# The filter taps' rests, last samples and sums as products of 128 rows and 128 columns

## The chip, the core and the metric

The kernel runs on one core of one Trainium2 chip. The metric is the device time of one execution in microseconds, as the median of several runs. The engines are named as in the profile: PE is TensorE's matrix products, PEld its weight loads, DVE is VectorE, ACT ScalarE, POOL GpSimd, and SP the queue that starts most of the DMAs.

## The reference: what is computed

The program is one layer with two half feed-forward blocks and two token mixers between them. The change touches the Hyena mixer's filters: a small network gives, for each of 512 positions, two orders and two directions, 512 channels. They are windowed, the second direction is turned round, and the whole is divided by its sum of absolute values over all positions.

```python
def hyena_kernels(l, w1, b1, fr1, w2, b2, fr2, w3):
    t, z = hyena_pos_features(l)
    h = jnp.sin(fr1 * (z @ w1 + b1))
    h = jnp.sin(fr2 * (h @ w2 + b2))
    h = (h @ w3).astype(jnp.float32).reshape(l, HYENA_ORDER, 2, B_WIDTH)
    ...
    h = h * window[:, None, None, :]
    kern = jnp.concatenate([h[:, :, 0], jnp.flip(h[:, :, 1], axis=0)], axis=0)
    return kern / (jnp.sum(jnp.abs(kern), axis=0, keepdims=True) + HYENA_L1_EPS)
```

Everything else (the feed-forward blocks, the recurrence, the convolution itself) is the same before and after.

## The kernel before

**Numbers in two parts.** Nearly every product is made from operands that are split into a rounded part (`hi`, made by ACT at line 127) and the rest (`lo`, made by DVE at line 128). `mm3` (lines 255 to 258) multiplies hi by hi, hi by lo and lo by hi. In the profile's rows a product reads `out<-moving,stationary`, then the stationary block's rows and columns, then the moving operand's rows and columns.

**The filter generator.** `filters()` makes four passes, one for each half of the channels (256) and each order. The last network layer has only 64 inputs, so its two parts lie one below the other in one tile: rows 0 to 63 of `h2s` are the rounded part of the activations and rows 64 to 127 their rest. The weights `w3r` are loaded twice, below each other, and rounded to `w3h`. So one product of 128 rows gives (hi + rest) times `w3h` (line 671). The weights' own rest `w3l` is only made for rows 0 to 63 (line 661), and a second product of 64 rows adds hi times `w3l` (line 672). Positions are dealt out to four quarters: position 4m + j is column m of `h2s[:, j]`, shifted by 4.

Each pass goes through four quarters. A quarter has four products of `taps` (two directions, lines 671 and 672 each), into one PSUM buffer `ps_w` (written `ps("ps_w3")` in the code). DVE multiplies them by the window (`hw`, line 679), POOL forms sum and difference of the two directions (`pm`, lines 683 and 684), ACT takes absolute values (line 685), POOL adds them up in `ab` (line 689; the buffer's name in the rows is `hw`), and the quarter before is split into `ahi` and `alo`.

The second direction is shifted by one position, so that its last sample (position 511) falls off the four quarters. After the quarters it is made apart: the two products again with a single stationary column (`slice(131, 132)`), which give one row `pl[0:1]` (`ps_last`). DVE multiplies it by the window's last row (line 698), ACT takes the absolute value (line 699): `la`, one row.

The column sum (lines 703 and 704) multiplies `ab` by a block of ones, and adds `la` by a product of one row. DVE inverts it, and the transform of the taps follows (`ps_k`, 36 products of 128 rows and 256 columns per pass, with the table `ft` stationary).

**The order.** The kernel is written as generators that yield a guess of their cost. A `Clock` interleaves `filters()` with the first feed-forward block, `ffn0()`, whose products (`ps_gl`, `ps_gc`, `ps_dl`, `ps_dc`) fill the time in which the vector engines work on a quarter. A scheduler then orders each engine's instructions, with a time model of its own. All PSUM tiles rotate through eight buffers; `la` and `wl` are tiles of the group `c1`, which rotates through seven.

After `ffn0()` come the context's norm (`context_norm`, lines 393 to 423), woven into the projections of the mixers (`ps_w`).

Of the kernel before, what the change touches and what calls it, by code (L numbers as in the profile page):

```python
# [10 lines left out]
F32 = mybir.dt.float32  # L11
# [4 lines left out]
ALU = mybir.AluOpType  # L16
# [3 lines left out]
P = 128  # L20
# [63 lines left out]
def layer_kernel(ctx: ExitStack, tc: tile.TileContext, a: dict, out: bass.AP):  # L84
    nc = tc.nc
    V, A, G, PE = nc.vector, nc.scalar, nc.gpsimd, nc.tensor
# [4 lines left out]
    mx = ctx.enter_context(tc.tile_pool(name="mx", bufs=1))  # L91
# [4 lines left out]
    def ps(name):  # L96
        return psp.tile([P, 512], F32, tag="ps", name=name, bufs=8)
# [16 lines left out]
    def c2(name, dims, dt=F32):  # L114
        return mx.tile([P] + dims, dt, tag="c2", name=name, bufs=15)
# [4 lines left out]
    def load(dst, src):  # L120
        nc.sync.dma_start(out=dst, in_=src)
# [4 lines left out]
    def split(hi, lo, x, eng=V):  # L126
        A.copy(hi, x)  # L127
        return eng.tensor_tensor(out=lo, in0=x, in1=hi.bitcast(F32), op=ALU.subtract)  # L128

    def raw_tile(name):  # L130
        return wp.tile([P, 1024], F32, tag="wraw", name=name, bufs=3)
# [144 lines left out]
    ones = const.tile([P, P], F32, name="ones")  # L276
# [11 lines left out]
    h2s = const.tile([P, 4, 132], F32R, name="h2s")  # L288
# [349 lines left out]
    def filters():  # L638
        ftab = forward_table()
        worder = [(hh, q) for hh in range(2) for _ in range(2) for q in range(4)]  # L640

        def window():
            win = c2("win", [2, 256])
            load(win, a["win"][worder.pop(0)])
            return win

        for hh, o in ((0, 0), (0, 1), (1, 0), (1, 1)):
            cs = slice(hh * 256, hh * 256 + 256)
            raw = raw_tile("w3r")
            w3r = raw[:, 0:512].rearrange("p (d c) -> p d c", d=2)  # L650
            for half in range(2):
                load(w3r[64 * half:64 * half + 64], a["hy_w3"][:, 2 * o:2 * o + 2, cs])
            hyb = c1("hyb", [256])
            load(hyb, a["hy_bias"][o, cs].partition_broadcast(P))
            wl = mx.tile([1, 256], F32, tag="c1", name="wl", bufs=7)
            load(wl, a["win_last"][:, cs])
            win = window()
            yield 0.0, 5.0
            w3h, w3l = (c2(n, [2, 256], F32R) for n in ("w3h", "w3l"))
            A.copy(w3h, w3r)  # L660
            V.tensor_tensor(out=w3l[0:64], in0=w3r[0:64], in1=w3h[0:64].bitcast(F32), op=ALU.subtract)
            V.tensor_scalar_mul(out=hyb, in0=hyb, scalar1=1.0 / 512.0)
            yield 0.0, 1.5
            ahi, alo = (c8(n, [2, 4, 256], F32R) for n in ("ahi", "alo"))
            ab = late = None

            def taps(p_, q, d, last=False):

                j, m = (q, 4) if d == 0 else ((q + 3) % 4, 4 - (q == 0))
                t = slice(131, 132) if last else slice(m, m + P)  # L670
                PE.matmul(p_, h2s[:, j, t], w3h[:, d], start=True, stop=False)
                PE.matmul(p_, h2s[0:64, j, t], w3l[0:64, d], start=False, stop=True)

            for q in range(4):
                p_ = ps("ps_w3")
                taps(p_[:, 0:256], q, 0)
                taps(p_[:, 256:512], q, 1)
                hw = c2("hw", [2, 256])
                V.tensor_tensor(out=hw, in0=p_.rearrange("p (d c) -> p d c", d=2), in1=win, op=ALU.mult)
                if q < 3:  # L680
                    win = window()
                pm = c2("pm", [2, 256])
                G.tensor_tensor(out=pm[:, 0], in0=hw[:, 0], in1=hw[:, 1], op=ALU.add)
                G.tensor_tensor(out=pm[:, 1], in0=hw[:, 0], in1=hw[:, 1], op=ALU.subtract)
                A.activation(hw, hw, AF.Abs)
                if q == 0:
                    ab = hw
                else:
                    G.tensor_tensor(out=ab, in0=hw, in1=ab, op=ALU.add)
                if late:  # L690
                    split(ahi[:, :, q - 1], alo[:, :, q - 1], late)
                late = pm
                yield 0.45, 3.0
            G.tensor_tensor(out=ab[:, 0], in0=ab[:, 0], in1=ab[:, 1], op=ALU.add)
            pl = ps("ps_last")
            taps(pl[0:1, 0:256], 0, 1, last=True)
            la = mx.tile([1, 256], F32, tag="c1", name="la", bufs=7)
            V.tensor_tensor(out=la, in0=pl[0:1, 0:256], in1=wl, op=ALU.mult)
            A.activation(la, la, AF.Abs)
            split(ahi[:, :, 3], alo[:, :, 3], late)  # L700
            yield 0.3, 5.0
            pn = ps("ps_l1")
            PE.matmul(pn[:, 0:256], ones, ab[:, 0], start=True, stop=False)
            PE.matmul(pn[:, 0:256], ones[0:1, :], la, start=False, stop=True)
            ri = c1("ri", [256])
            V.tensor_scalar(out=ri, in0=pn[:, 0:256], scalar1=EPS, scalar2=512.0, op0=ALU.add, op1=ALU.mult)
            V.reciprocal(out=ri, in_=ri)
            rib = ri.unsqueeze(1).broadcast_to([P, 2, 256])
            yield 0.9, 0.0
            te, to, tw = (c4(n, [2, 2, 256]) for n in ("te", "to", "tw"))  # L710
            ep = None
            fl = lambda x: x.rearrange("p d c -> p (d c)")

            def pool(out_, x, y, op):
                G.tensor_tensor(out=out_, in0=x, in1=y, op=op)

            def keep(fam, x):
                nc.gpsimd.dma_start(out=k_dram[o, hh, fam], in_=fl(x))

            for t, k, q, turned in ((te, 0, 0, 0), (te, 1, 2, 0), (to, 0, 1, 0), (to, 1, 3, 0), (tw, 0, 1, 1), (tw, 1, 3, 1)):  # L720
                p_ = ps("ps_k")
                for c in range(2):
                    mm3([p_[:, c * 256:c * 256 + 256]], *ftab(q, c ^ turned), [(ahi[:, c, q], alo[:, c, q])], True, True)
                V.tensor_tensor(out=t[:, k], in0=p_.rearrange("p (d c) -> p d c", d=2), in1=rib, op=ALU.mult)
                if t is te and k == 0:
                    pool(te[:, 0, 0], te[:, 0, 0], hyb, ALU.add)
                elif t is te:
                    ep = c2("ep", [2, 256])
                    pool(fl(ep), fl(te[:, 0]), fl(te[:, 1]), ALU.add)
                    pool(fl(te[:, 1]), fl(te[:, 0]), fl(te[:, 1]), ALU.subtract)  # L730
                elif t is to and k == 1:
                    pool(fl(to[:, 0]), fl(to[:, 0]), fl(to[:, 1]), ALU.add)
                    pool(fl(to[:, 1]), fl(ep), fl(to[:, 0]), ALU.add)
                    keep(0, to[:, 1])
                    pool(fl(te[:, 0]), fl(ep), fl(to[:, 0]), ALU.subtract)
                    keep(1, te[:, 0])
                elif t is tw and k == 1:
                    pool(tw[:, 0, 0], tw[:, 0, 0], tw[:, 1, 0], ALU.subtract)
                    pool(tw[:, 0, 1], tw[:, 1, 1], tw[:, 0, 1], ALU.subtract)
                    pool(fl(tw[:, 1]), fl(te[:, 1]), fl(tw[:, 0]), ALU.add)  # L740
                    keep(2, tw[:, 1])
                    pool(fl(te[:, 1]), fl(te[:, 1]), fl(tw[:, 0]), ALU.subtract)
                    keep(3, te[:, 1])
                yield 0.65, 0.0
# [534 lines left out]
    for i in range(4):  # L1279
        whi, wlo = weights()  # L1280
        for k2 in range(2):
            dm = 2 * i + k2
            p_ = ps("ps_pa")
# [11 lines left out]
    for half, s in enumerate(HS):  # L1295
# [3 lines left out]
        for n, dm in enumerate(range(KT) if half == 0 else (6, 7, 0, 1, 2, 3, 4, 5)):  # L1299
# [5 lines left out]
            p_ = ps("ps_out")  # L1305
# [82 lines left out]
    for gi, (f0, f1) in enumerate(GROUPS1):  # L1388
# [21 lines left out]
        if gi < len(GROUPS1) - 1:  # L1410
            lx = [[x] for x in ml]
            for dm in range(KT):
                pl = ps("ps_dl")
# [16 lines left out]
        for half, s in enumerate(HS):  # L1430
# [4 lines left out]
            for n, dm in enumerate(range(KT) if half == 0 else (6, 7, 0, 1, 2, 3, 4, 5)):  # L1435
                pl = ps("ps_dl")
# [13 lines left out]
def _constants():  # L1450
    f32 = np.float32
    p = np.arange(512, dtype=f32)
    t = p / f32(511)
# [4 lines left out]
    z = np.concatenate([t[:, None], np.cos(ang), -np.sin(ang)], axis=-1).astype(f32)  # L1458
    dmax, dmin = math.log(1e-2) / 0.3, math.log(1e-2) / 1.5
    deltas = np.abs(np.linspace(dmin, dmax, 512, dtype=f32))  # L1460
    win = (np.exp(-t[:, None] * deltas[None, :]) + f32(0.05)).astype(f32)
    shifted = np.concatenate([np.zeros((1, 512), f32), win[:-1]], axis=0)

    wv = np.stack([win, shifted]).reshape(2, 128, 4, 2, 256)
    wv = wv.transpose(3, 2, 1, 0, 4)
# [4 lines left out]
    dft = np.stack([  # L1470
        np.concatenate([g(x).T for x in ang for g in (np.cos, np.sin)], axis=1),
        np.concatenate([np.cos(x) for x in ang] + [np.sin(x) for x in ang], axis=1),
        np.concatenate([np.cos(x) for x in mirror] + [-np.sin(x) for x in mirror], axis=1)]).astype(f32)
# [7 lines left out]
    x = s[:, None] ^ s[None, :]  # L1481
    masks = np.stack([(x >> l) == 1 for l in range(7)], axis=1).astype(f32)
    return {
        "zT": z.T, "win": wv, "win_last": win[511:512], "dft": dft,
        "pos_r": er.T.reshape(4, 128, 8).transpose(1, 0, 2), "pos_c": ec.T.reshape(4, 128, 64).transpose(1, 0, 2),
        "masks": masks.reshape(128, 896), "ident": np.eye(128, dtype=f32),
    }
# [66 lines left out]
```

## Time and profile before

| | |
|---|---|
| median of 3 runs | 1526.18 us (1524.2 to 1526.97) |
| the profiled execution, own time | 1524.52 us |
| its span, first to last instruction | 1522.7 us |
| PE busy | 1479.5 us (97%), 8776 products |
| DVE busy | 1034.9 us (68%), 1553 instructions |
| ACT busy | 556.4 us (37%) |
| POOL busy | 305.1 us (20%) |

Busy time of an engine is the time in which at least one of its records runs. Records of neighbouring products overlap, so the distance between two starts says what a product takes from PE, and not its duration.

### The profile page before, as it was taken

Reading aid. Unit: us, or ns where it says so; the run is one execution under the profiler, and the core shown is the slowest. Engines: PE = TensorE matmul, PEld = TensorE weight load, DVE = VectorE, ACT = ScalarE, POOL = GpSimd, SP = SyncE. Lnnn points to the kernel's source line nnn. Section 1 sums busy time; section 2 is a strip of 40 time slices with the busy share of each in tenths; the row PEclk is TensorE's granted clock in tenths of the full one; section 3 lists DMA queues with packets and bytes.
Section 4 is the critical chain, followed back from the end, with each engine's and each line's share of the span. In section 5 each row is a group of like instructions: output and inputs, shape, how many; then the busy total and the mean of one; then the engine's idle time right before and its main releaser. Section 6 shows DMA issues by size and latency. Waiting matters only on the chain. (4 is left out here: it accounts for less than half of the span.)

```text
span 1522.7 us, 22141 instructions
## 1 busy us (share of the span) xinstructions
PE 1479.5 (97%) x8776; PEld 1297.0 (85%) x8776; DVE 1034.9 (68%) x1553; ACT 556.4 (37%) x947; POOL 305.1 (20%) x248
## 2 busy tenths in 40 slices
PE   8899999999999999999999999999998999999997
PEld 4698888888888888878888888888798989899896
DVE  6937984565455554585876756885757768779686
ACT  5442122212322332454433334444433525435253
POOL 1400110010254464000000021232531002212020
PEclk9999999999999999999999999999999999999998
DMA  8334574463232332424442421124532132333322
GB/s 333 131 108 135 186 236 163 137 230 101 76 103 85 114 101 87 151 97 152 160 150 92 136 86 50 63 91 167 203 122 84 49 119 98 95 100 97 112 84 84
DMA packets 69705, 188.93 MB, mean 124 GB/s; under 512 B 7836, under 2 KB 16800, under 8 KB 69345
## 3 DMA queue, kind: packets, MB, share of 16 engines
q1 hardware_dynamic: 58608, 152.61, 30.6%
q0 software_dynamic: 9408, 33.70, 6.6%
q8 instruction: 69, 1.13, 0.3%
q10 hardware_dynamic: 1584, 1.20, 0.2%
q14 instruction: 36, 0.29, 0.1%
HBM read 169.92 MB, written 17.56 MB: 123 GB/s over the span
## 5 line engine op out<-in xcount | busy, mean ns | idle before, releaser
L127 ACT CAST whi<-wraw 128x1024 fp32r<-128x1024 f32 (+3 forms) x188 | 171.1, 911 | 484.8 <-PE ps_gc L256 178.5
L128 DVE TENSOR_TENSOR wlo<-wraw,whi 128x1024 fp32r<-128x1024 f32 (+3 forms) x136 | 156.5, 1152 | 136.4 <-ACT whi L127 136.4
L255 PE MATMUL ps_gl<-nhi,whi 128*128 128x512 f32 x360 | 143.8, 399 | 0.0
L255 PE MATMUL ps_w<-nhi,whi 128*128 128x512 f32 x352 | 141.4, 402 | 1.3 <-ACT th L951 1.1
L258 PE MATMUL ps_w<-nhi,wlo 128*128 128x512 f32 x352 | 138.6, 394 | 3.3 <-DVE wlo L128 3.3
L258 PE MATMUL ps_gl<-nhi,wlo 128*128 128x512 f32 x360 | 141.6, 393 | 0.0
L256 PE MATMUL ps_gl<-nlo,whi 128*128 128x512 f32 x360 | 141.5, 393 | 0.0
L256 PE MATMUL ps_w<-nlo,whi 128*128 128x512 f32 x352 | 138.5, 393 | 0.0
L128 POOL TENSOR_TENSOR wlo<-wraw,whi 128x1024 fp32r<-128x1024 f32 x25 | 62.1, 2485 | 377.1 <-ACT whi L127 364.4
L256 PE MATMUL ps_dl<-mid,whi 128*128 128x512 f32 (+1 forms) x321 | 123.7, 386 | 0.0
L258 PE MATMUL ps_dl<-mid,wlo 128*128 128x512 f32 (+1 forms) x321 | 123.5, 387 | 0.0
L255 PE MATMUL ps_dl<-mid,whi 128*128 128x512 f32 (+1 forms) x321 | 123.3, 389 | 0.0
L255 PE MATMUL ps_gc<-chi,whi 128*128 128x258 f32 x328 | 93.5, 286 | 7.0 <-ACT chi L127 6.7
L333 DVE SCALAR_TENSOR_TENSOR junk<-wmod,cvb 128x1024 f32<-128x1024 f32 x80 | 97.7, 1222 | 2.0 <-DMA wmod<-in_mod_w 0.8
L256 PE MATMUL ps_gc<-clo,whi 128*128 128x258 f32 x328 | 93.6, 285 | 0.0
L258 PE MATMUL ps_gc<-chi,wlo 128*128 128x258 f32 x328 | 93.1, 284 | 0.0
L1380 POOL TENSOR_TENSOR u<-p,res 128x512 f32<-128x512 f32 x18 | 33.0, 1834 | 284.2 <-ACT p L1375 140.7
L255 PEld LDWEIGHTS ps_gl<-nhi,whi 128*128 128x128 f32 x360 | 67.6, 188 | 17.7 <-ACT bias L809 0.8
L255 PEld LDWEIGHTS ps_gc<-chi,whi 128*128 128x128 f32 x328 | 62.4, 191 | 20.6 <-ACT chi L127 7.1
L258 PEld LDWEIGHTS ps_w<-nhi,wlo 128*128 128x128 f32 x352 | 66.5, 189 | 15.7 <-DVE wlo L128 3.7
L255 PEld LDWEIGHTS ps_w<-nhi,whi 128*128 128x128 f32 x352 | 66.7, 189 | 14.7 <-ACT th L951 1.4
L343 POOL DMA_DIRECT2D wmod<-in_mod_w x56 | 29.6, 529 | 238.3 <-DVE junk L333 197.4
(460 smaller groups left out, 4107.5 us busy)
## 6 DMA issues: line engine op xcount, KB each, us to landing
wmod<-in_mod_w POOLq DMA_DIRECT2D x56, 512.0 KB, 4.3
wraw<-in_wg SPq DMA_DIRECT2D x44, 512.0 KB, 3.7
wraw<-in_wu SPq DMA_DIRECT2D x44, 512.0 KB, 3.5
wraw<-in_w_in SPq DMA_DIRECT2D x44, 512.0 KB, 3.2
wraw<-in_wd SPq DMA_DIRECT2D x40, 384.0 KB, 3.5
wm<-in_mod_w SPq DMA_DIRECT2D x16, 512.0 KB, 8.3
wraw<-in_wd SPq DMA_DIRECT2D x19, 320.0 KB, 3.3
win<-in_win SPq DMA_DIRECT2D x16, 256.0 KB, 3.4
```

The lines of the kernel that those rows point to most:

```text
L127: A.copy(hi, x)
L128: return eng.tensor_tensor(out=lo, in0=x, in1=hi.bitcast(F32), op=ALU.subtract)
L255: PE.matmul(o, whi, xhi, start=first, stop=False)
L256: PE.matmul(o, whi, xlo, start=False, stop=False)
L258: PE.matmul(o, wlo, xhi, start=False, stop=last)
L333: return V.scalar_tensor_tensor(out=junk[:, 0:1024], in0=raw, scalar=1.0, in1=cvb[:, i], op0=ALU.mult, op1=ALU.mult, accum_out=res)
L343: nc.gpsimd.dma_start(out=raw[i % 3], in_=a["mod_w"][8 * tiles[i][0] + tiles[i][1]])
L1380: G.tensor_tensor(out=u57, in0=p57, in1=res[:, 1:2].broadcast_to([P, 2, 256]), op=ALU.add)
```

## The change

It has five parts.

- `w3l` gets rows 64 to 127 too. DVE fills them with `w3h - w3h`, that is with zeros (a second instruction of 64 rows and 512 columns per pass). The second product of `taps` then runs over all 128 rows; the zeros meet the rest rows of `h2s`.
- The last sample is made with the 128 columns that end in it (`m = 4` for the fourth quarter), so the product gives 128 rows, the last of which is the sample.
- `win_last` gets 31 rows of zeros ahead of the window's last row, and `wl` is loaded into partitions 96 to 127. `la` lives in the same buffer: rows 96 to 127 of the product times `wl` leave one row that is not zero.
- DVE adds `la` to rows 96 to 127 of `ab`.
- The column sum is then one product; the one of a single row goes.

```diff
-            wl = mx.tile([1, 256], F32, tag="c1", name="wl", bufs=7)
-            load(wl, a["win_last"][:, cs])
+            wl = c1("wl", [256])
+            load(wl[96:128], a["win_last"][:, cs])
...
             V.tensor_tensor(out=w3l[0:64], in0=w3r[0:64], in1=w3h[0:64].bitcast(F32), op=ALU.subtract)
+            V.tensor_tensor(out=w3l[64:128], in0=w3h[64:128].bitcast(F32), in1=w3h[64:128].bitcast(F32), op=ALU.subtract)
...
-                j, m = (q, 4) if d == 0 else ((q + 3) % 4, 4 - (q == 0))
-                t = slice(131, 132) if last else slice(m, m + P)
-                PE.matmul(p_, h2s[:, j, t], w3h[:, d], start=True, stop=False)
-                PE.matmul(p_, h2s[0:64, j, t], w3l[0:64, d], start=False, stop=True)
+                j, m = (q, 4) if d == 0 else ((q + 3) % 4, 4 - (q == 0 and not last))
+                PE.matmul(p_, h2s[:, j, m:m + P], w3h[:, d], start=True, stop=False)
+                PE.matmul(p_, h2s[:, j, m:m + P], w3l[:, d], start=False, stop=True)
...
-            taps(pl[0:1, 0:256], 0, 1, last=True)
-            la = mx.tile([1, 256], F32, tag="c1", name="la", bufs=7)
-            V.tensor_tensor(out=la, in0=pl[0:1, 0:256], in1=wl, op=ALU.mult)
+            taps(pl[:, 0:256], 0, 1, last=True)
+            la = wl[96:128]
+            V.tensor_tensor(out=la, in0=pl[96:128, 0:256], in1=la, op=ALU.mult)
             A.activation(la, la, AF.Abs)
+            V.tensor_tensor(out=ab[96:128, 0], in0=ab[96:128, 0], in1=la, op=ALU.add)
...
-            PE.matmul(pn[:, 0:256], ones, ab[:, 0], start=True, stop=False)
-            PE.matmul(pn[:, 0:256], ones[0:1, :], la, start=False, stop=True)
+            PE.matmul(pn[:, 0:256], ones, ab[:, 0], start=True, stop=True)
...
-        "win_last": win[511:512],
+        "win_last": np.concatenate([np.zeros((31, 512), f32), win[511:512]], axis=0),
```

The scheduler's order follows. The last entry of a row is the shape of the instruction's output, so the 64 rows of a product don't appear in it. On PE, at the first pass's column sum, the feed-forward's last product, the sum (`ps_l`) and the transform's first products stood before as

```order
L258 MATMUL ps_gl<-nhi,wlo 128x512
L258 MATMUL ps_gc<-chi,wlo 128x258
L703 MATMUL ps_l_3509<-hw,ones 128x256
L704 MATMUL ps_l_3509<-la,ones 128x256
L255 MATMUL ps_k<-ahi,ft 128x256
L256 MATMUL ps_k<-alo,ft 128x256
```

and stand now as

```order
L258 MATMUL ps_gl<-nhi,wlo 128x512
L258 MATMUL ps_gc<-chi,wlo 128x258
L705 MATMUL ps_l_3510<-hw,ones 128x256
L255 MATMUL ps_k<-ahi,ft 128x256
L256 MATMUL ps_k<-alo,ft 128x256
```

The row of line 704 is gone and nothing else moved there; in the third and fourth pass the sum also stands three feed-forward products later. On DVE, in the third pass, from the last sample's multiply to the column sum's first use (`ri`), there stood before

```order
L698 TENSOR_TENSOR la<-ps_last,wl 1x256
L128 TENSOR_TENSOR wlo<-wraw,whi 128x1024
L450 SCALAR_TENSOR_TENSOR md<-ps_gl,bias,sg 128x512
L450 SCALAR_TENSOR_TENSOR md<-ps_gc,bias,sg 128x256
L128 TENSOR_TENSOR mid<-md,mid 128x512
L128 TENSOR_TENSOR mid<-md,mid 128x256
L706 TENSOR_SCALAR ri<-ps_l_4423 128x256
```

and there stands now

```order
L699 TENSOR_TENSOR wl<-ps_last,wl 32x256
L128 TENSOR_TENSOR wlo<-wraw,whi 128x1024
L450 SCALAR_TENSOR_TENSOR md<-ps_gl,bias,sg 128x512
L450 SCALAR_TENSOR_TENSOR md<-ps_gc,bias,sg 128x256
L701 TENSOR_TENSOR hw<-hw,wl 32x256
L128 TENSOR_TENSOR mid<-md,mid 128x512
L128 TENSOR_TENSOR mid<-md,mid 128x256
L707 TENSOR_SCALAR ri<-ps_l_4424 128x256
```

The new add (line 701, `hw` is the buffer of `ab`) stands behind the hidden layer's two products; in the first pass it stands directly behind the multiply, in the second behind one cast of weights, in the fourth as here. On DVE at the context's norm, after the filters, the reciprocal of the norm (`rr`) and its diagonal (`dg`) stood before as

```order
L964 SCALAR_TENSOR_TENSOR cv<-ps_w,sm,cv 128x511
L400 RECIPROCAL rr<-rr 128x2
L402 TENSOR_TENSOR dg<-ident,rr 128x256
L128 TENSOR_TENSOR wlo<-wraw,whi 128x1024
L962 SCALAR_TENSOR_TENSOR cv<-ps_w,sm,cv 128x511
```

and stand now as

```order
L965 SCALAR_TENSOR_TENSOR cv<-ps_w,sm,cv 128x511
L128 TENSOR_TENSOR wlo<-wraw,whi 128x1024
L400 RECIPROCAL rr<-rr 128x2
L402 TENSOR_TENSOR dg<-ident,rr 128x256
L963 SCALAR_TENSOR_TENSOR cv<-ps_w,sm,cv 128x511
```

A cast of weights moved ahead of the reciprocal; PE's products for the sum of squares stand six projection products later there.

## Rows read from the trace of the kernel before

**Rows 1.** The page's busy line: us, share of the span, instructions.

```profile
PE 1479.5 (97%) x8776; PEld 1297.0 (85%) x8776; DVE 1034.9 (68%) x1553; ACT 556.4 (37%) x947; POOL 305.1 (20%) x248
```

**Rows 2.** Stretches: us, busy PE, PEld, DVE, ACT, POOL, clock, DMA share, GB/s.

```profile
395.00:580.00 185.00, 185.00 (x1035) 155.07 (x1034) 100.96 (x133) 50.92 (x95) 94.53 (x92) 1.00 0.29 92
640.00:700.00 60.00, 56.51 (x299) 48.24 (x298) 46.26 (x72) 32.03 (x52) 3.08 (x2) 0.97 0.37 121
```

**Rows 3.** Timeline of PE, first column sum: start us, us, instruction, count.

```profile
427.06 0.38 PE L703 MATMUL ps_l<-hw,ones 128*128 128x256 f32 x1
...
427.27 0.38 PE L703 MATMUL ps_l<-hw,ones 128*128 128x256 f32 x1
...
427.58 0.69 PE L704 MATMUL ps_l<-la,ones 1*128 1x256 f32 x2
428.20 0.39 PE L255 MATMUL ps_k<-ahi,ft 128*128 128x256 f32 x1
428.43 0.28 PE L256 MATMUL ps_k<-alo,ft 128*128 128x256 f32 x1
428.55 0.28 PE L258 MATMUL ps_k<-ahi,ft 128*128 128x256 f32 x1
```

**Rows 4.** Timeline of PE and PEld around the first quarter's taps.

```profile
398.16 0.28 PE L258 MATMUL ps_gc<-chi,wlo 128*128 128x258 f32 x1
...
398.29 0.28 PE L671 MATMUL ps_w<-w3h,h2s 128*128 128x256 f32 x1
398.49 0.18 PEld L672 LDWEIGHTS ps_w<-w3l,h2s 64*128 64x128 f32 x1
398.49 0.38 PE L672 MATMUL ps_w<-w3l,h2s 64*128 64x256 f32 x1
...
398.80 0.38 PE L671 MATMUL ps_w<-w3h,h2s 128*128 128x256 f32 x1
...
399.12 0.38 PE L672 MATMUL ps_w<-w3l,h2s 64*128 64x256 f32 x1
...
399.43 0.50 PE L255 MATMUL ps_gl<-nhi,whi 128*128 128x512 f32 x1
...
399.77 0.40 PE L256 MATMUL ps_gl<-nlo,whi 128*128 128x512 f32 x1
...
400.00 0.28 PE L255 MATMUL ps_gc<-chi,whi 128*128 128x258 f32 x1
```

**Rows 5.** Timeline of PE around the first last sample.

```profile
420.22 0.28 PE L671 MATMUL ps_last<-w3h,h2s 128*1 128x256 f32 x1
...
420.63 0.50 PE L255 MATMUL ps_gl<-nhi,whi 128*128 128x512 f32 x1
```

**Rows 6.** The tile w3l: ns least/median/most, first and last start in us.

```profile
L661 DVE TENSOR_TENSOR w3l<-w3r,w3h x4: 677/1080/1084, 390.1 to 536.4; 64x512 fp32r<-64x512 f32 x4
```

**Rows 7.** Timeline of DVE (two quarters' multiplies; third pass) and PE's third column sum.

```profile
411.56 0.68 DVE L679 TENSOR_TENSOR hw<-ps_w,win 128x512 f32<-128x512 f32 x1
...
416.26 0.68 DVE L679 TENSOR_TENSOR hw<-ps_w,win 128x512 f32<-128x512 f32 x1
...
522.97 0.41 DVE L698 TENSOR_TENSOR la<-ps_last,wl 1x256 f32<-1x256 f32 x1
...
525.32 0.47 DVE L450 SCALAR_TENSOR_TENSOR md<-ps_gc,bias,sg 128x256 f32<-128x256 f32 x1
...
529.19 0.59 PE L703 MATMUL ps_l<-hw,ones 128*128 128x256 f32 x2
```

**Rows 8.** Timeline of PE after the filters; the bracket is idle time and its releaser.

```profile
656.52 0.50 PE L258 MATMUL ps_w<-nhi,wlo 128*128 128x512 f32 x1 [3.26 <-DVE wlo L128]
...
657.67 0.63 PE L255 MATMUL ps_w<-nhi,whi 128*128 128x512 f32 x1
658.10 0.63 PE L256 MATMUL ps_w<-nlo,whi 128*128 128x512 f32 x1
...
660.23 0.63 PE L255 MATMUL ps_w<-nhi,whi 128*128 128x512 f32 x1
```

More of the change, by code (lines that the diff above doesn't have):

```diff
@@ L1483, in _constants @@
     return {
-        "zT": z.T, "win": wv, "win_last": win[511:512], "dft": dft,
+        "zT": z.T, "win": wv, "win_last": np.concatenate([np.zeros((31, 512), f32), win[511:512]], axis=0), "dft": dft,
         "pos_r": er.T.reshape(4, 128, 8).transpose(1, 0, 2), "pos_c": ec.T.reshape(4, 128, 64).transpose(1, 0, 2),
```

## The prediction

> **What bounds the kernel now.** I read the busy line of the page first: TensorE (PE) is busy for 97% of the span, VectorE (DVE) for 68% [rows 1]. That is an average, so I then read the stretch that the change touches. The four passes of the filter generator run between 395 and 580 us, woven into the first feed-forward block. There PE is busy for 185.00 of 185.00 us at the full granted clock, 1.00, which is the 2.4 GHz level, and DVE for 100.96 us [rows 2]. Nothing that PE does there waits, so what PE spends there is spent by the kernel, as long as nobody else becomes late.
>
> A PE that is always "busy" can still be slow, because the records of neighbouring products overlap. So I read the starts, not the durations. A product of 128 rows with 256 columns moving follows its neighbour after 0.12 us (428.43 to 428.55) even though every one of them loads a new stationary block [rows 3]. A product of 512 columns takes 0.23 us (399.77 to 400.00) [rows 4]. Around the taps the steps are different. The rest product (line 672, 64 rows) starts 0.20 us after its partner, the next two follow at 0.31 and 0.32 us, the ordinary product after them at 0.31 us, and even the one behind that comes after 0.34 instead of 0.23 us [rows 4]. The weight-load row shows how: the load of line 672 starts at 398.49, with its own product, so nothing of it lies under the product before. I read that as PE emptying itself, and loading in the open, at each change between 64 and 128 rows.
>
> **The change part by part.** All sums are made on PE's starts in the profiled execution (1524.52 us).
>
> Taps: four products per quarter, 16 quarters (4 passes of 4). Now: 398.29 to 399.43 is 1.14 us, plus 0.34 - 0.23 = 0.11 us that the next product loses, 1.25 us [rows 4]. With all four of 128 rows I take the 0.12 us of the transform's products (ps_k), which change the stationary block in just this way, twice the same and then another: 4 x 0.12 = 0.48 [rows 3]. Saved 0.77 us, times 16 = **12.3 us**.
>
> Last samples: two products, four times. Now 420.22 to 420.63, 0.41 us, and the next one is again a record of 0.50 us like that at 399.43, so the same 0.11 us: 0.52 [rows 4, 5]. After: 2 x 0.12 = 0.24. That 128 stationary columns are loaded where one was, the 0.12 us already holds. Saved 0.28 x 4 = **1.1 us**.
>
> Sums: line 703 issues two PE instructions and line 704, of one row, two more. From 427.06 to 428.20 is 1.14 us, and the product behind loses 0.23 - 0.12 = 0.11: 1.25 us [rows 3]. Line 704 goes altogether. What is left are two instructions 0.21 us apart (427.06, 427.27): 0.42. Saved 0.83 x 4 = **3.3 us**. If the step to the next product stays exposed, this is 0.4 us less (4 x 0.11).
>
> Together 16.7 us.
>
> What is added lies elsewhere. DVE gets a second half of w3l per pass, on 64 rows like the first, 0.68 to 1.08 us [rows 6]; the first tap product is at 398.29 and the existing half is done by 391, so 7 us hide it. DVE also gets the add of `la` into rows 96 to 127 of `ab`, which I take as 0.41 us like the multiply before it (the bounds are that and the 0.47 us of the update next to it [rows 7]). That is at most 4 x (1.08 + 0.47) = 6.2 us on an engine with 84 us idle in the stretch: nothing on the path, and 6.2 us only if DVE were the bound. The load of `win_last` carries 32 rows instead of one, is one DMA as before, at the same place of SP's queue and a pass ahead of its use: nothing. ScalarE's Abs covers 32 rows instead of one with the same 256 columns, 0.40 us: the same.
>
> The add is a new wait. DVE holds still for ScalarE's Abs and for GpSimd's sum over the two directions, and the casts of weights queue behind it. And PE's column sum now waits for the add, where it waited for the Abs. In the third pass the scheduler puts the add behind two hidden-layer products: the second of them starts at 525.32 and lasts 0.47 us, so the add ends near 526.2, and PE arrives at 529.19 [rows 7]. That leaves 3.0 us, the least I find. The earlier taps bring PE there sooner but the whole chain begins sooner too, since it begins with the taps.
>
> What is late next is that chain. From the multiply of one quarter to that of the next, queued on DVE behind the low half of the quarter before, it took 411.56 to 416.26, 4.70 us [rows 7]. PE's period per quarter is 24 ordinary products, half of them at 0.23 and half at 0.12 us, which is 4.2 us, and the taps' 1.25: 5.45, and it falls by 0.77 to 4.68. They become level. PE does not wait for the chain at each quarter, only for a PSUM buffer of eight, so I put it at nothing; its price is a rival below.
>
> The scheduler also moves things where it need not: around 660 to 690 us, in the context's norm, the cast of a weight now stands ahead of DVE's reciprocal, and PE gives out six more projection products before the sum of squares. The size of such a shuffle I bound by the one stall that stands there now: 3.26 us of waiting for a weight's low half, then seven products (657.67 to 660.23) 0.43 us apart instead of 0.23, PE at its lower level of 1.2 GHz after having stood idle [rows 8]; the granted clock of 640 to 700 is 0.97 for it [rows 2]. 3.26 + 7 x 0.20 = 4.7 us, won or lost. I take zero: the casts move ahead of PE's need, not behind it.
>
> One rule speaks against all this. The Trainium skill (TensorE: Matmul & The Clock Gate, Why this matters for your kernels) says that a single product of 32 rows takes the same time as one of 128, so filling rows should give nothing. By that rule only line 704's eight instructions go, at 0.21 us each 1.7 us; by the rows here it is 16.7 us, and I go by the rows, since here the 64-row products stand among 128-row ones.
>
> **The rivals.**
>
> A. *Rows are not the reason.* The gaps would belong to the slices of `h2s` or to loading the same block twice, and only line 704 goes: between 8 x 0.21 = 1.7 and 3.3 us, so 1522.9 to 1524.5 us. Against it: the first product of line 671 has the same slice and starts 0.13 us after its neighbour [rows 4], and ps_k loads the same block twice at 0.12. Chance 0.04.
>
> B. *The vector chain takes over.* If PSUM buffers come free too late, PE runs at the chain's pace, and where other DVE work stretches that from 4.70 to 5.45 us or more, the 12.3 us of the taps are given back: 1526.2 - 4.4 = 1521.8. Against it: DVE is idle 45% of the stretch [rows 2] and four quarters are too few to use up eight buffers. Chance 0.04; a part of it, up to 5 us, lies in the range.
>
> C. *PE waits for the new add.* This is the one that ends slower. If the add lands behind a late cast, PE stands before each column sum, and comes back at its lower clock, at the 4.7 us of [rows 8]: four places, 18.8 us against 16.7, 1528.3 us. It decides from a wait of 16.7 / 4 = 4.2 us per place, so the add must come 3.0 + 4.2 = 7.2 us later than the rows have it. Chance 0.03.
>
> D. *The shuffle of the context's norm counts.* Loss of up to 4.7 us: up to 1514.2, chance 0.13. Gain of as much, the stall goes: down to 1504.8, chance 0.08.
>
> **How the numbers follow.** The forecast, 16.7 us off, has 0.68. The profiled execution would go from 1524.52 to 1507.8 us; it is a fast one of the kernel, 1.7 us under the median of 1526.18, and I take the same gain off the median: 1509.5 us. Its own spread is the 0.4 us of the column sums and the 1.4 us by which half the runs differ. The range goes down to rival D's gain, 1504.8, and up to D's loss with the 0.4 us, 1514.6. Left out are A, B and C with 0.11 together. A measurement of this kernel can tell about 0.2%, 3 us, from no change, so faster means under 1523.1. Faster: the forecast, D and B, 0.93; same: A, 0.04; slower: C, 0.03.
>
> **What would show it.** The tap products 0.12 us apart and none of the following products late; two instructions instead of four at the column sum, the product behind them 0.21 us later; 395 to 580 shortened by about 16 to 17 us, with PE busy throughout and its clock at 1.00; DVE's add done before PE arrives. Wrong would be: 64-row gaps that stay (A), PE idle with PSUM or DVE as the releaser in this stretch (B, C), or a difference that sits at 640 to 700 us (D).

## The result, and the profile after

The changed kernel takes 1506.54 us (median of 4 runs, 1506.00 to 1507.06) where the kernel before takes 1525.19 us beside it (median of 4, 1523.45 to 1526.97). The ratio is 0.9878, with a 95% interval of 0.9861 to 0.9895: 18.6 us less, between 16.0 and 21.2. A second measurement of the same two kernels gave 1506.85 against 1524.4 us, 0.9886 [0.9869, 0.9902]: 17.4 us less. Both intervals hold the forecast gain of 16.7 us. The time itself was forecast at 1509.5 us, 3.0 us above what was measured: 1.0 us of that is that the kernel before took 1525.19 us here and not the 1526.18 that I started from, and 1.9 us is gain beyond the forecast. The profiled execution took 1506.39 us, its span is 1504.6 us, 18.1 us shorter than before.

The busy line of the page (us, share of the span, instructions) answers [rows 1]:

```profile
PE 1462.1 (97%) x8768; PEld 1291.8 (86%) x8768; DVE 1043.2 (69%) x1561; ACT 556.4 (37%) x947; POOL 309.0 (21%) x248
```

PE has eight instructions fewer, the two of line 704 in each of four passes. It is busy 17.4 us less, and its share is still 97%: what went was time that counted as busy. DVE has eight instructions more, the two added ones of each pass.

Two stretches (us, then busy PE, PEld, DVE, ACT, POOL, granted clock, DMA share, GB/s) answer [rows 2]. The filters' stretch ends about 17 us earlier now, so its window is 395 to 565, and that of the norm is moved with it:

```profile
395.00:565.00 170.00, 170.00 (x1036) 152.01 (x1035) 108.21 (x142) 52.15 (x96) 98.60 (x93) 1.00 0.32 100
620.00:685.00 65.00, 62.40 (x338) 53.63 (x337) 50.11 (x77) 34.91 (x56) 3.97 (x2) 0.97 0.38 124
```

In the filters PE is still busy without a gap, at the same granted clock of 1.00 (its 2.4 GHz level). DVE went from 100.96 us in 185 to 108.21 in 170, and PE did not wait for it.

The timeline of PE at the first quarter's taps (start us, us, instruction) answers [rows 4]; line 671 of before is 672 now, 672 is 673:

```profile
397.89 0.28 PE L672 MATMUL ps_w<-w3h,h2s 128*128 128x256 f32 x1
398.01 0.28 PE L673 MATMUL ps_w<-w3l,h2s 128*128 128x256 f32 x1
398.13 0.28 PE L672 MATMUL ps_w<-w3h,h2s 128*128 128x256 f32 x1
398.25 0.28 PE L673 MATMUL ps_w<-w3l,h2s 128*128 128x256 f32 x1
398.37 0.40 PE L255 MATMUL ps_gl<-nhi,whi 128*128 128x512 f32 x1
398.60 0.39 PE L256 MATMUL ps_gl<-nlo,whi 128*128 128x512 f32 x1
```

The four products start 0.12 us apart, and the second ordinary one behind them follows after 0.23 us. From the first tap to that one it was 1.48 us and is 0.71: 0.77 us less, as forecast. The other quarters are alike: over all 16 it was 23.7 us and is 11.25.

The same view at the first last sample, which answers [rows 5], and at the first column sum, which answers [rows 3]:

```profile
416.67 0.28 PE L672 MATMUL ps_last<-w3h,h2s 128*128 128x256 f32 x1
416.78 0.28 PE L673 MATMUL ps_last<-w3l,h2s 128*128 128x256 f32 x1
...
417.14 0.39 PE L256 MATMUL ps_gl<-nlo,whi 128*128 128x512 f32 x1
...
423.23 0.59 PE L705 MATMUL ps_l<-hw,ones 128*128 128x256 f32 x2
423.48 0.47 PE L255 MATMUL ps_k<-ahi,ft 128*128 128x256 f32 x1
423.78 0.27 PE L256 MATMUL ps_k<-alo,ft 128*128 128x256 f32 x1
```

The last sample with what follows it takes 0.47 us, where it took 0.75 (0.41 and 0.34): 0.28 less. From the sum's start to the transform's second product it is 0.55 us, and was 1.37 (427.06 to 428.43): 0.82 less. One sign that I had named looks different: the transform's first product comes 0.25 us after the sum's start and not 0.42, and the second 0.30 us after the first. Only the distance to the second is what the sum of the prediction gives (0.42 and 0.12).

After the filters, the stall of [rows 8] stands at 638.65:

```profile
638.65 0.50 PE L258 MATMUL ps_w<-nhi,wlo 128*128 128x512 f32 x1 [2.44 <-DVE wlo L128]
```

It is 2.44 us instead of 3.26. That this isn't the change's doing is shown below, with the second execution.

### The profile page after: what moved, and what is told of

Read it like the earlier page. It is cut to its first block, busy times and chain, and to the rows that moved or that the text cites. A ratio compares the mean times of both kernels' runs of the same rounds, so it can differ in the third digit from the quotient of the medians.

```text
span 1504.6 us, 22134 instructions
## 1 busy us (share of the span) xinstructions
PE 1462.1 (97%) x8768; PEld 1291.8 (86%) x8768; DVE 1043.2 (69%) x1561; ACT 556.4 (37%) x947; POOL 309.0 (21%) x248
```

## The experiments

My theory was that each change between a product of 128 rows and one of 64 (or of one) costs PE time of its own, that the number of changes sets the price, and that DVE's added work lies beside it. The rivals were that the gaps belong to the taps' slices and only line 704 counts, that DVE or the new wait takes a part back, and that the gain lies in the shuffle after the filters.

Where a ratio is given, the gain in us is worked out from it; the two medians can lie up to 1 us beside it. A time from one run is given as it is, and what is read from such a run are its rows.

### One part alone: the quarters' taps

```diff
+            V.tensor_tensor(out=w3l[64:128], in0=w3h[64:128].bitcast(F32), in1=w3h[64:128].bitcast(F32), op=ALU.subtract)
...
-                PE.matmul(p_, h2s[0:64, j, t], w3l[0:64, d], start=False, stop=True)
+                if last:
+                    PE.matmul(p_, h2s[0:64, j, t], w3l[0:64, d], start=False, stop=True)
+                else:
+                    PE.matmul(p_, h2s[:, j, t], w3l[:, d], start=False, stop=True)
```

> The kernel before with one part of the change alone: the rests of the quarters' taps get zero rows and run over 128 rows; the last sample (64 rows, one column) and the column sum (with its product of one row) stay. Theory (a product of fewer than 128 rows makes PE empty itself and load in the open): the four tap products 0.12 us apart, 0.77 us less per quarter, 16 x 0.77 = 12.3 us less than before, about 1513; the column sum still takes 1.37 us from its first start to the second transform product. Rival A (the rows are not the reason): the tap products keep their steps of 0.2 to 0.3 us and the time stays within 1 us of before.

Measured: 1512.86 us (4 runs) against 1523.57 us (13 runs), ratio 0.9924 [0.9909, 0.9938], 11.6 us less [9.4, 13.9]. The timeline of PE in this kernel (rest products are line 676, the sum's first product 707 here):

```profile
397.84 0.28 PE L672 MATMUL ps_w<-w3h,h2s 128*128 128x256 f32 x1
...
398.54 0.39 PE L256 MATMUL ps_gl<-nlo,whi 128*128 128x512 f32 x1
...
423.45 0.59 PE L707 MATMUL ps_l<-hw,ones 128*128 128x256 f32 x2
...
424.82 0.28 PE L256 MATMUL ps_k<-alo,ft 128*128 128x256 f32 x1
```

From the first tap to the second ordinary product it is 0.70 us, as in the changed kernel (0.71); from the sum to the transform's second product still 1.37. The interval holds the forecast term of 12.3 us. So the slices and the twice loaded block (rival A) are not the reason: they are unchanged here, and the gaps are gone with the 64 rows. PE, DVE, ScalarE and GpSimd have their instructions in the order of before in this kernel, at the norm too, but for the four that write the zeros, so this gain owes nothing to a new order.

### The other part alone: the sum, with rests of 64 rows

The edit goes from the changed kernel back; the last sample keeps its 128 columns.

```diff
-            V.tensor_tensor(out=w3l[64:128], in0=w3h[64:128].bitcast(F32), in1=w3h[64:128].bitcast(F32), op=ALU.subtract)
...
-                PE.matmul(p_, h2s[:, j, m:m + P], w3l[:, d], start=False, stop=True)
+                PE.matmul(p_, h2s[0:64, j, m:m + P], w3l[0:64, d], start=False, stop=True)
```

> The changed kernel with the taps' rests put back to 64 rows (quarters and last sample; the last sample keeps its 128 columns), so that only the one column sum with DVE's add is left of the change. Theory: 4 x 0.83 = 3.3 us less than before, about 1522, and the tap quarters take 1.48 us from the first product to the second ordinary one, as before. Rival C (PE waits for the new add): PE idle ahead of the column sum, and no gain or a loss. If much more than 3.3 us is gained, the 1.4 us that the changed kernel gained beyond the 16.7 us belong to the add and the sum.

Measured: 1520.51 us (10 runs) against 1523.57 us, ratio 0.9981 [0.9971, 0.9991], 2.9 us less. The quarters take 1.48 us, as before. PE did not wait for the new add, and not much more than the term of 3.3 us was gained, so the add and the sum don't hold the 1.4 us beyond the forecast. A part that goes the other way lies at the last sample, on PE's timeline of this kernel and, below it, of before:

```profile
419.59 0.28 PE L671 MATMUL ps_last<-w3h,h2s 128*128 128x256 f32 x1
419.80 0.38 PE L672 MATMUL ps_last<-w3l,h2s 64*128 64x256 f32 x1
420.11 0.50 PE L255 MATMUL ps_gl<-nhi,whi 128*128 128x512 f32 x1
420.45 0.39 PE L256 MATMUL ps_gl<-nlo,whi 128*128 128x512 f32 x1
```

```profile
420.43 0.28 PE L672 MATMUL ps_last<-w3l,h2s 64*1 64x256 f32 x1
...
420.97 0.39 PE L256 MATMUL ps_gl<-nlo,whi 128*128 128x512 f32 x1
```

It takes 0.86 us where it took 0.75 with one column (420.22 to 420.97), 0.11 more, four times, which makes 2.8 us of the term of 3.3. The step from the 64-row product to the next is 0.31 us with 128 columns (419.80 to 420.11) and was 0.20 with one (420.43 to 420.63 in [rows 5]). I read the 0.11 us as the load of a block of 64 rows and 128 columns that lies under no other product; with one column it is next to nothing. The interval, 1.4 to 4.4 us, is too wide to show 0.4 us by itself; the row shows it.

### The sum with its second product kept, over 128 rows

```diff
-            load(wl[96:128], a["win_last"][:, cs])
+            load(wl, a["win_last"][:, cs])
...
-            la = wl[96:128]
-            V.tensor_tensor(out=la, in0=pl[96:128, 0:256], in1=la, op=ALU.mult)
+            la = wl
+            V.tensor_tensor(out=la, in0=pl[:, 0:256], in1=la, op=ALU.mult)
             A.activation(la, la, AF.Abs)
-            V.tensor_tensor(out=ab[96:128, 0], in0=ab[96:128, 0], in1=la, op=ALU.add)
...
-            PE.matmul(pn[:, 0:256], ones, ab[:, 0], start=True, stop=True)
+            PE.matmul(pn[:, 0:256], ones, ab[:, 0], start=True, stop=False)
+            PE.matmul(pn[:, 0:256], ones, la, start=False, stop=True)
...
-        "zT": z.T, "win": wv, "win_last": np.concatenate([np.zeros((31, 512), f32), win[511:512]], axis=0), "dft": dft,
+        "zT": z.T, "win": wv, "win_last": np.concatenate([np.zeros((127, 512), f32), win[511:512]], axis=0), "dft": dft,
```

> The changed kernel, but the last sample stays a tile of its own: 128 rows (127 of them zero by the window), added by a second product of 128 rows in the column sum, as before by one of one row; DVE's add goes. It parts what line 704 cost as two more instructions from what it cost by having one row. Theory: two more instructions of 0.21 us at each of four places, 0.42 us each, 1.7 us slower than the changed kernel, about 1508; from the sum's first start to the second transform product 0.55 + 0.42 = 0.97 us, against 1.37 with the row of one. Rival (the rows don't count, the product itself costs): 1.37 us again and 3.3 us slower, about 1510.

Measured: 1509.58 us (4 runs) against 1523.57, ratio 0.9904 [0.9889, 0.9919], 14.6 us less [12.3, 16.9]. That holds both what was expected, 1.7 us less gain than the forecast's 16.7, and its rival, 3.3 less; the rows tell the two apart. PE's timeline at the first sum:

```profile
423.14 0.59 PE L704 MATMUL ps_l<-hw,ones 128*128 128x256 f32 x2
423.57 0.59 PE L705 MATMUL ps_l<-wl,ones 128*128 128x256 f32 x2
...
424.12 0.28 PE L256 MATMUL ps_k<-alo,ft 128*128 128x256 f32 x1
```

0.98 us, against 1.37 before and 0.55 after, and 0.97 were expected. Of the 0.82 us that the sum gave, 0.43 were the second product's two instructions, and 0.39 were that it had one row. The added DVE instruction, which the changed kernel has and this one has not, is worth its place: without it a second product must be paid for.

### Fewer changes of row count

In the kernel before, the second direction's rest goes ahead of its main product, so that the rows run 128, 64, 64, 128: two changes instead of four, the same products.

```diff
-                PE.matmul(p_, h2s[:, j, t], w3h[:, d], start=True, stop=False)
-                PE.matmul(p_, h2s[0:64, j, t], w3l[0:64, d], start=False, stop=True)
+                pair = [(h2s[:, j, t], w3h[:, d]), (h2s[0:64, j, t], w3l[0:64, d])]
+                if d == 1 and not last:
+                    pair = pair[::-1]
+                PE.matmul(p_, *pair[0], start=True, stop=False)
+                PE.matmul(p_, *pair[1], start=False, stop=True)
```

> The kernel before, all products of 64 rows as they are, but in each quarter the second direction's rest product stands ahead of its main product, so that the rows go 128, 64, 64, 128 instead of 128, 64, 128, 64: two changes of rows in a quarter instead of four. If the change of rows is what costs: the step from rest to rest is 0.12 us like any other, the steps are 0.20, 0.12, 0.31, then 0.23 to the ordinary product: 0.86 us where 1.25 were, 16 x 0.39 = 6.2 us less than before. If a product of fewer rows costs by itself (its load never lies under another product): the step from rest to rest is 0.22 to 0.31 us and 3.2 to 4.6 us are gained.

Measured in one run: 1517.45 us against one of 1526.27 us, 8.8 us where 6.2 were expected; a pair of single runs can't size a difference of 2.6. Over the 16 quarters PE's timeline gives 6.2 us (23.7 us before, 17.5 here, from the first tap to the second ordinary product). At the first quarter it reads:

```profile
397.47 0.28 PE L674 MATMUL ps_w<-w3h,h2s 128*128 128x256 f32 x1
397.67 0.38 PE L675 MATMUL ps_w<-w3l,h2s 64*128 64x256 f32 x1
397.90 0.27 PE L674 MATMUL ps_w<-w3l,h2s 64*128 64x256 f32 x1
398.10 0.39 PE L675 MATMUL ps_w<-w3h,h2s 128*128 128x256 f32 x1
398.32 0.40 PE L255 MATMUL ps_gl<-nhi,whi 128*128 128x512 f32 x1
398.56 0.40 PE L256 MATMUL ps_gl<-nlo,whi 128*128 128x512 f32 x1
```

The four take 0.85 us to the ordinary product, which then loses nothing to the next (0.24). The total was expected at 0.86. How it is spread was expected otherwise: the steps are 0.20, 0.23, 0.20 and 0.22 us, not one of 0.12 between the rests and one of 0.31 behind them. By itself the 0.23 us between the two rests is what the other theory of the expectation gives, that a product of 64 rows costs by itself. The weight loads in the same stretch decide:

```profile
397.67 0.18 PEld L675 LDWEIGHTS ps_w<-w3l,h2s 64*128 64x128 f32 x1
397.78 0.19 PEld L674 LDWEIGHTS ps_w<-w3l,h2s 64*128 64x128 f32 x1
398.10 0.19 PEld L675 LDWEIGHTS ps_w<-w3h,h2s 128*128 128x128 f32 x1
```

At the two changes (397.67 and 398.10) the load starts with its own product, in the open. The load of the second rest starts at 397.78, 0.12 us ahead of its own product and under the first rest, which the other theory ruled out. The record of a product whose load lies in the open begins with that load, so that the load's 0.11 us shows in the step behind it. A change then is 0.08 us ahead of the record and 0.11 us behind it, which gives all the steps: 0.12 and 0.08 are 0.20, 0.12 and 0.11 are 0.23, and in [rows 4], where one change follows another, 0.12, 0.11 and 0.08 are 0.31. So the price belongs to the change. Together: four changes cost 1.25 us a quarter, two 0.85, none 0.48, which is 0.19 to 0.20 us for each.

### Rows or columns: 128 rows, but one column at the last sample

The kernel before with rests of 128 rows everywhere; the last sample stays one column, and the sum as it was.

```diff
+            V.tensor_tensor(out=w3l[64:128], in0=w3h[64:128].bitcast(F32), in1=w3h[64:128].bitcast(F32), op=ALU.subtract)
...
-                PE.matmul(p_, h2s[0:64, j, t], w3l[0:64, d], start=False, stop=True)
+                PE.matmul(p_, h2s[:, j, t], w3l[:, d], start=False, stop=True)
```

> The kernel before with all rest products over 128 rows, the last sample's too, but the last sample keeps its single stationary column; the column sum is as before. It parts rows from columns. If only rows count: the two last-sample products 0.12 us apart, the next one 0.12 us later and not late itself (0.47 us from the first to the second ordinary product), 12.3 + 1.1 us less than before. If columns count too: the 0.75 us of before stay, at least in part.

Measured in one run: 1511.3 us against 1526.27 us, 15.0 us where 13.4 were expected, again a pair of single runs. PE's timeline at the first last sample:

```profile
416.08 0.27 PE L672 MATMUL ps_last<-w3h,h2s 128*1 128x256 f32 x1
416.19 0.28 PE L673 MATMUL ps_last<-w3l,h2s 128*1 128x256 f32 x1
...
416.54 0.40 PE L256 MATMUL ps_gl<-nlo,whi 128*128 128x512 f32 x1
```

0.46 us, as with 128 columns (0.47). Where the rows stay at 128, a stationary block of one column costs nothing and saves nothing; the rows alone made the gap. The changed kernel needs its 128 columns for another reason, to have the sample in a row that can be added to `ab`.

### Is 128 needed: rests of 96 rows

The changed kernel, with 32 rows of zeros instead of 64.

```diff
-            V.tensor_tensor(out=w3l[64:128], in0=w3h[64:128].bitcast(F32), in1=w3h[64:128].bitcast(F32), op=ALU.subtract)
+            V.tensor_tensor(out=w3l[64:96], in0=w3h[64:96].bitcast(F32), in1=w3h[64:96].bitcast(F32), op=ALU.subtract)
...
-                PE.matmul(p_, h2s[:, j, m:m + P], w3l[:, d], start=False, stop=True)
+                PE.matmul(p_, h2s[0:96, j, m:m + P], w3l[0:96, d], start=False, stop=True)
```

> The changed kernel, but the rest products run over 96 rows (32 zero rows below the rests) instead of 128, in the quarters and the last sample. It asks whether any row count below 128 costs, or only that of a smaller group of rows. If any: the quarters take 1.25 us as before (1.48 from the first product to the second ordinary one), 12.3 us and 4 x 0.39 us slower than the changed kernel, about 1520. If only half the rows or less cost: 0.48 us (0.71) and the time of the changed kernel.

Measured in one run: 1507.03 us, beside 1506.85 us for the changed kernel on the same chip. PE and PEld in the first quarter:

```profile
397.36 0.28 PE L672 MATMUL ps_w<-w3h,h2s 128*128 128x256 f32 x1
397.48 0.28 PE L673 MATMUL ps_w<-w3l,h2s 96*128 96x256 f32 x1
397.59 0.28 PE L672 MATMUL ps_w<-w3h,h2s 128*128 128x256 f32 x1
```

```profile
397.36 0.19 PEld L673 LDWEIGHTS ps_w<-w3l,h2s 96*128 96x128 f32 x1
```

Products of 96 rows stand 0.12 us apart among those of 128, and the load of 96 rows starts at 397.36, with the product before its own. In [rows 4] the load of 64 rows starts with its own product. So it isn't "fewer than 128 rows" that is paid for. Of the row counts tried here, 64 and one cost a change and 96 does not; 32 was not tried.

### DVE's added work in half: one subtraction for all rows

```diff
-            V.tensor_tensor(out=w3l[0:64], in0=w3r[0:64], in1=w3h[0:64].bitcast(F32), op=ALU.subtract)
-            V.tensor_tensor(out=w3l[64:128], in0=w3h[64:128].bitcast(F32), in1=w3h[64:128].bitcast(F32), op=ALU.subtract)
+            V.tensor_tensor(out=w3l, in0=w3r, in1=w3h.bitcast(F32), op=ALU.subtract)
```

> The changed kernel, but the rests' lower half is not zeros: one DVE instruction of 128 rows makes w3r - w3h for both halves, so the second product also adds rest times rest. One DVE instruction of 0.7 to 1.1 us less per pass, same products. Theory (DVE is not the bound there): the same time as the changed kernel within 1 us. Rival (the longer DVE chain costs something): up to 4 x 1.08 = 4.3 us faster than the changed kernel.

Measured: 1507.64 us (4 runs) against 1523.57, ratio 0.9893 [0.9878, 0.9908], inside the intervals of the changed kernel and not below its time (1506.54 and 1506.85). One DVE instruction less per pass is worth nothing that shows, where up to 4.3 us would have been won if DVE bounded this stretch. This version computes the same as the changed kernel but for the product of the two rests, which it adds.

### The changed kernel again

> The changed kernel itself, in more rounds beside the kernel before on one chip, to size the gain. The steps on PE give 16.7 us. If that is all, the ratio is near 0.989; if the 1.4 us more of the first trace (0.4 us ahead of the taps, 0.8 us of a shorter stall in the norm) come with the change, it is near 0.988.

Measured: the 1506.85 us and 0.9886 given above, 17.4 us less. Its stall after the filters:

```profile
639.43 0.73 PE L258 MATMUL ps_w<-nhi,wlo 128*128 128x512 f32 x1 [3.26 <-DVE wlo L128]
```

It is 3.26 us, the stall of the kernel before, in a kernel that otherwise showed 2.44. So those 0.8 us differ between two executions of the same code. The ratio lies between the two that were expected, 0.989 for the steps alone and 0.988 for all of the first trace.

## Why the prediction held, point by point

**PE is the bound of the stretch.** PE was busy throughout it before and after, and the two larger terms, measured on its starts, came out in the time of a run that has each alone (11.6 us for 12.3; 2.9 us for 2.8, the last samples' loss taken off). The 1.1 us of the last samples show in the rows only; no run has them alone.

**The three terms.** Taps 0.77 us forecast and 0.77 found, 16 times, 12.3 us; alone they gave 11.6 [9.4, 13.9]. Last samples 0.28 and 0.28. Sums 0.83 and 0.82, so that the 0.4 us that stood in doubt did not come. Together 16.7 us in the trace. What made these numbers good was to take starts to the second ordinary product behind a group, since the first one's record begins with its load, and 0.11 us of the price stand behind it.

**What is above 16.7.** The first pair of traces differs by 18.1 us. Of the 1.4 us beyond the forecast, 0.8 are the stall, which the repeat showed to come and go. Another 0.4 lie ahead of the taps, in code that is the same: PE's first product of the filter network (line 603) comes at 366.4 us before, at 366.0 in the changed kernel and at 365.4 in its 96-row version. Up to there these three issue the same, and they stand up to 1 us apart. The last 0.2 us lie behind the norm. In the repeat's trace the stall is as long as before, and yet its span is as short as in the first, 1504.7 us: what the stall took came back between 1026 and 1184 us, far behind the change, and I did not follow that to a cause. So the 1.4 us are no part of the change that the runs would show; they are of the size by which executions of one kernel differ.

**Rows are the reason (against rival A).** Shown three ways: the gaps go with the rows alone, a block of one column does not bring them back, and with half the changes, at the same number of 64-row products, half of what can be won is won. The rule that I weighed (the Trainium skill, TensorE: Matmul & The Clock Gate, Why this matters for your kernels: a single product of 32 rows takes as long as one of 128) would have given 1.7 us; the time disagrees with reading it so for 64 rows between products of 128. Another page fits better (the Trainium skill, TensorEngine Tiling (Array Packing), Key Properties: changing the tiling mode drains TensorE). It gives no price; here it is 0.19 to 0.20 us with a block of 128 columns, and 0.14 on the mean of the two changes where the 64-row block has one column.

**The added DVE work is hidden.** It is, but one size was off. I bounded the zeros by 1.08 us; the tile view of after has up to 1.68 (median 1.67):

```profile
L663 DVE TENSOR_TENSOR w3l<-w3h x4: 690/1674/1679, 390.4 to 525.3; 64x512 fp32r<-64x512 f32 x4
```

The add was 0.42 us for 0.41. The bound of 6.2 us for both was too low: four times 1.68 and 0.42 are 8.4, and DVE's busy time on the page rose by 8.3.

**The slack of the new wait.** This is the step that failed, without a cost. I wrote that 3.0 us were the least, because PE and the chain would both come sooner. The rows of after, DVE and PE in the third and in the fourth pass:

```profile
515.79 0.42 DVE L701 TENSOR_TENSOR hw<-hw,wl 32x256 f32<-32x256 f32 x1
...
517.65 0.60 PE L705 MATMUL ps_l<-hw,ones 128*128 128x256 f32 x2
...
557.60 0.42 DVE L701 TENSOR_TENSOR hw<-hw,wl 32x256 f32<-32x256 f32 x1
...
558.33 0.60 PE L705 MATMUL ps_l<-hw,ones 128*128 128x256 f32 x2
```

The add ends at 516.21 and PE comes 1.4 us later; in the fourth pass it ends at 558.02 and PE comes 0.3 us later. In the run of the sum alone, where PE, DVE, ScalarE and GpSimd have the order of the changed kernel but for the zeros, and the rests have 64 rows, the fourth pass reads

```profile
568.21 0.42 DVE L700 TENSOR_TENSOR hw<-hw,wl 32x256 f32<-32x256 f32 x1
...
572.16 0.60 PE L704 MATMUL ps_l<-hw,ones 128*128 128x256 f32 x2
```

which is 3.5 us. So the taps that became faster took the slack, with the zeros beside them: in the run with one subtraction, without the zeros' instruction, it is 0.8 us. PE gains on the chain within a pass, and what stands at the chain's end, the add, is what it gains on. The chain of the multiplies of the fourth pass now reads

```profile
544.28 0.68 DVE L680 TENSOR_TENSOR hw<-ps_w,win 128x512 f32<-128x512 f32 x1
...
549.89 0.68 DVE L680 TENSOR_TENSOR hw<-ps_w,win 128x512 f32<-128x512 f32 x1
```

which is 5.61 us, and the two intervals ahead of it are 5.95 and 5.30, while PE's taps follow each other at 4.7 us, as forecast. So PE and the chain are not level there: the multiply starts 0.2 us behind the start of the product that follows its taps in the first quarter, and 2.9 us behind it in the fourth. The 4.70 us that I took for the chain's period was one interval of the old trace; the others there are 5.1 to 8.1 us, most of them near PE's own pace of 5.5, so that the old trace could not show by them what the chain needs.

Rival B's condition, a chain of 5.45 us or more, was thus met in this pass, and its price was not paid: PE shows no gap in the stretch. That fits the reason the prediction gave, that four quarters are too few to use up eight buffers. Rival C was three tenths of a microsecond from beginning, though far from its price: it needed 4.2 us at each sum to decide. I expect a further cut of PE's work in this stretch to meet that wait, in the fourth pass first; no run tried one.

**The shuffle at the norm (rival D).** Nothing of it shows but the stall that comes and goes: 2.44 us in three of the ten traces and 3.26 to 3.28 in the others, that of before among them. The run of the sum alone has the changed kernel's order at the norm. It gained 2.9 us [1.4, 4.4], where its sums and last samples account for 2.8, so neither a gain nor a loss of 4.7 us hides there.

## What to carry to other kernels

Read PE by its starts, to the second product behind the group in question: a PE that is 100% busy at its full clock can hold gaps of 0.2 us at each place where the products change between 64 rows, or one, and 128. Where few rows stand among many, fill them with zeros, or put the narrow ones side by side, before counting instructions; the fill need not reach 128, since 96 rows were as good here. And when the bound is cut, don't take the slack of the chain beside it from the old trace: a slack shrinks by what the bound gains on the chain, and a chain that keeps up with a slow bound shows the bound's period and not its own.

## What the runs showed of the hardware

A change between products of 64 and of 128 rows, with 128 columns to load, costs 0.19 to 0.20 us at a granted clock of 1.00. Of that 0.11 us is a load of 128 columns in the open (with one column the step is shorter by that much), so that some 0.08 us are left, which I read as PE emptying itself; no run shows that part by itself. Between 96 and 128 rows there is no such price (0.12 us from start to start), and between two products of 64 rows the load lies under the first of them (397.78 us in the run with two changes).

Where an instruction of DVE and one of GpSimd meet, either can be the longer one, in the same kernel. After the filters, DVE's eight instructions of line 417 and GpSimd's first split beside the last of them, in the timelines of the changed kernel's first execution and of its second:

```profile
626.54 5.39 DVE L417 SCALAR_TENSOR_TENSOR mt<-hl,m_lat,r 128x512 f32<-128x512 f32 x8 [0.38 <-ACT r L412]
630.64 2.45 POOL L128 TENSOR_TENSOR nlo<-mt,nhi 128x512 fp32r<-128x512 f32 x1 [52.31 <-ACT nhi L127]
```

```profile
626.50 6.44 DVE L417 SCALAR_TENSOR_TENSOR mt<-hl,m_lat,r 128x512 f32<-128x512 f32 x8 [0.38 <-ACT r L412]
630.60 1.79 POOL L128 TENSOR_TENSOR nlo<-mt,nhi 128x512 fp32r<-128x512 f32 x1 [52.31 <-ACT nhi L127]
```

Once GpSimd takes 2.45 us and DVE 5.39, once GpSimd 1.79 and DVE 6.44; the difference on DVE is all in the last of the eight, 0.75 or 1.79 us. With DVE slower, the cast that PE waits for comes later (638.16 us instead of 637.38), and the stall is 3.26 us instead of 2.44. The ten traces go together in this: three have the long split and the stall of 2.44, seven, that of before among them, have the long DVE instruction and a stall of 3.26 to 3.28. What decides between the two is not shown.
